# Hybrid encoder trunk on one core: split weight tiles kept in DRAM, sample attention in a pipelined order, another order at the start and at the end

## The chip, the cores and the metric

The kernel runs on one NeuronCore of one Trainium2 chip. The metric is device time in microseconds for one execution; the time before is 3031.82 us, the median of three runs (3031.12 to 3034.32). Matmuls run on TensorE (PE; its weight loads are shown as PEld), elementwise work on VectorE (DVE), ScalarE (ACT) and GpSimd (POOL). All DMAs are issued by SyncE (SP), from one queue that is worked off in order, and run on 16 DMA engines.

## The reference

One layer is computed for two groups of requests that share the weights: a prompt of 2048 tokens and a sample of 8 x 16 tokens, each of the latter with 1024 cached keys and values. All of it is in 32-bit floats.

```
h = rms_norm(x, norm_g)                                  # (tokens, 1024)
(a_x, a_b, a_c, a_z, g_q, g_f, g_i, g_z,
 s_q, s_k, s_v, s_z, m_a, m_b, m_c) = split_cols(h @ w_in)   # 12 x 512 + 3 x 1024 columns
o_a = a_b * conv3(a_c * a_x) * silu(a_z)                 # branch A: short causal convolution
o_b = rms_norm(hgrn_scan(g_q, f(g_f), k(g_f), g_i)) * silu(g_z)   # branch B: gated linear recurrence
q, k = rms_norm(s_q, q_norm_g), rms_norm(s_k, k_norm_g)  # per head, 8 heads of 64
z = q @ k.T / 8                                          # branch C: stick-breaking attention, strictly causal
A = sigmoid(z) * (product over later keys of sigmoid(-z))
o_c = (A @ v) * silu(s_z)
m = sigmoid(m_a) * (o_a @ wb_a) + sigmoid(m_b) * (o_b @ wb_b) + sigmoid(m_c) * (o_c @ wb_c)
y = x + m @ w_out
```

Outputs are y, the last convolution rows, the recurrent states, and the keys and values of both request groups.

## The kernel before

Tokens are cut into 17 tiles of 128: tile 0 is the sample, tiles 1 to 16 the prompt. The input projection goes over three token groups of 5, 6 and 6 tiles (`GROUPS`, L39), each in two chunks of at most 384 tokens. `run_jobs` (L1118) runs the same 64 jobs for each group. A job is one block of columns of w_in: a channel job (`chan_job`, L1000) has 128 columns, one weight part, and computes them channel by token (`proj_chan`, L581: 8 blocks of k, 3 matmuls each); a token job (`tok_job`, L993) has 256 columns in two parts (k blocks 0 to 3 and 4 to 7) and computes them token by channel (`proj_tok`, L593). Jobs of the first stretch alternate: one channel job, one token job of k, v or q.

**Three matmuls for a product.** Every operand is split (`split`, L174): ScalarE casts it to float32r (hi), VectorE subtracts that from the source (lo), and `PASS3` (L579) multiplies hi by hi, hi by lo and lo by hi. `wload` (L179) does this for weights: one DMA of 512 KB into a staging tile wst (2 buffers), then hi into whi and lo into wlo (3 buffers each). It is called one job ahead (L1132, L1133; L1269 to L1271 in the merge), and again for each token group, so the same 72 parts of w_in are loaded and split three times, and the 20 parts of w_branch and w_out four times.

**Start.** `Prepare` loads x, squares and sums a tile on ScalarE (`square`, L501), takes the inverse root on POOL (`rstd_of`, L192: a multiply-add and a pow), scales by it and by the gain g_bc on VectorE (`scale`, L508), transposes on TensorE and splits the result into hh and hl (`turn`, L512). For group 0 this is `first_steps` (L544). The DMA of g_bc (512 KB, broadcast to all partitions) is the first in the queue (L172). The lower bound of the forget gate (L641 to L655), seven level masks (L659 to L671) and two selectors (L808 to L815) are built at the start on POOL and VectorE.

**Keys and queries.** `post_qk` (L679) normalizes them, transposes into one PSUM bank (ps_hg, L148) and copies that on ScalarE to kt (one buffer, L701), which goes to DRAM.

**Background work.** Generators are stepped between the pieces of a job, by a budget of their yielded costs (`Background`, L58; rates at L45 to L48): the recurrence, the sample attention in group 1, the prompt attention in group 2 and the merge. The framework that turns this program into queues may also move an instruction ahead on its engine where its buffers are free.

**Sample attention** (`sample_attention`, L344): for each of 8 requests, three segments of keys, the last keys first. A segment loads 2 or 3 blocks of keys, transposes them (L405), forms z (L412), two sigmoids, the running product (scan, L424) and its product with sigmoid(z) (L426), transposes that (L429) and multiplies by the values (L447). All this stands in one row, segment after segment.

**Merge.** Four groups of tiles (`PGROUPS`, L41). For each, 12 branch jobs (`bjob`, L1200: branch x of 3, 256 output columns dp of 4) multiply by w_branch; the product is gated on VectorE (L1231, L1233), added on POOL (L1234) and, for x = 2, split into mh and ml. Four output jobs (`ojob`, L1239), each with two weight parts, multiply by w_out, add x and store y (L1253, L1254). The output jobs of a group alternate with the first four branch jobs of the next; those of the last group come alone at the end. Before the last branch, what is left of that group's attention is run out (L1207).

Of the kernel before, what the change touches and what calls it, by code (L numbers as in the profile page):

```python
# [11 lines left out]
I32 = mybir.dt.int32  # L12
# [86 lines left out]
def trunk(ctx: ExitStack, tc: tile.TileContext, x_prompt, x_sample, cache_conv, state_hgrn, cache_k, cache_v,  # L99
# [72 lines left out]
    nc.sync.dma_start(g_bc, norm_g[0].partition_broadcast(P))  # L172

    def split(hi, lo, src, eng=None):  # L174

        nc.scalar.copy(hi, src)  # L176
        (eng or nc.vector).tensor_tensor(lo, src, hi.bitcast(F32), ALU.subtract)  # L177

    def wload(pieces):  # L179

        out = []
        for v in pieces:
            a, b = v.shape[1], v.shape[2]
            st = wp.tile([P, a, b], F32, tag="wst", name="wst", bufs=2)
            nc.sync.dma_start(st, v)
            hi = wp.tile([P, a, b], F32R, tag="whi", name="whi")
            lo = wp.tile([P, a, b], F32R, tag="wlo", name="wlo")
            split(hi, lo, st)
            out.append((hi, lo))
        return out  # L190

    def rstd_of(ssq, n, count):  # L192

        v = small.tile([P, n], F32, tag=f"rv{n}", name="rv")
        nc.gpsimd.tensor_scalar(v, ssq, 1.0 / count, EPS, ALU.mult, ALU.add)
        r = small.tile([P, n], F32, tag=f"rr{n}", name="rr")
        nc.gpsimd.tensor_tensor(r, v, mhalf.broadcast_to([P, n]), ALU.pow)
        return r
# [58 lines left out]
    def attn_pair(m0, m1):  # L257
# [15 lines left out]
        for m in range(m0, m1):  # L273
# [8 lines left out]
            for i in range(nq):  # L282
# [61 lines left out]
    def sample_attention():  # L344
# [45 lines left out]
        for b in range(NB):  # L390
            pv = ps_pv()
            carry = one
            vnew = sa.tile([TS, 8, 64], F32, tag="vnew", name="vnew", bufs=1)
            nc.sync.dma_start(vnew, VV[b * TS:(b + 1) * TS])
            for sg in (2, 1, 0):
                nblk = 2 if sg == 2 else 3
                w = nblk * P + (TS if sg == 2 else 0)
                kt = sa.tile([P, 4, 384], F32, tag="kt", name="kt", bufs=2)
                for bi in range(nblk):
                    blk = 3 * sg + bi  # L400
                    kc = sa.tile([P, 512], F32, tag="cst", name="kc", bufs=3)
                    nc.sync.dma_start(kc, cache_k[0, b, blk * P:(blk + 1) * P].rearrange("t h d -> t (h d)"))
                    tp = ps_tp()
                    for h in range(4):
                        nc.tensor.transpose(tp[:, h * P:(h + 1) * P], kc[:, h * P:(h + 1) * P], idf)  # L405
                    nc.scalar.copy(kt[:, :, bi * P:(bi + 1) * P], tp.rearrange("p (h t) -> p h t", h=4))
                    yield 1.3
                z = ps_z()
                if sg == 2:
                    nc.tensor.matmul(z[:, 256:256 + TS], idb, nmask, start=True, stop=False, skip_group_check=True)  # L410
                for h in range(4):
                    nc.tensor.matmul(z[32 * h:32 * h + 32, :nblk * P], qz[:, h, b], kt[:, h, :nblk * P],  # L412
                                     start=sg != 2, stop=True, skip_group_check=True)
                if sg == 2:
                    for h in range(4):
                        nc.tensor.matmul(z[32 * h:32 * h + 32, 256:256 + TS], qz[:, h, b],
                                         knew[:, h, b * TS:(b + 1) * TS], start=False, stop=True,
                                         skip_group_check=True)
                nc.scalar.activation(sn[:, 384 - w:384], z[:, :w], AF.Sigmoid, scale=-0.125)
                sp = sa.tile([P, 384], F32, tag="sp", name="sp")  # L420
                nc.scalar.activation(sp[:, :w], z[:, :w], AF.Sigmoid, scale=0.125)
                pr = sa.tile([P, 385], F32, tag="pr", name="pr")
                s_in = sn[:, 384 - w:385][:, ::-1]
                nc.vector.tensor_tensor_scan(pr[:, 384 - w:385][:, ::-1], s_in, s_in, carry, ALU.mult, ALU.bypass)  # L424
                carry = pr[:, 384 - w:385 - w]
                nc.vector.tensor_tensor(sp[:, :w], sp[:, :w], pr[:, 385 - w:385], ALU.mult)  # L426
                tp = ps_tp()
                for bi in range(nblk):
                    nc.tensor.transpose(tp[:, bi * P:(bi + 1) * P], sp[:, bi * P:(bi + 1) * P], idf)  # L429
                at_ = sa.tile([P, 384], F32, tag="at", name="at_")  # L430
                if sg == 2:
                    nc.tensor.transpose(tp[0:TS, 256:384], sp[:, 256:256 + TS], idf)
                    nc.scalar.copy(at_[:, 0:256], tp[:, 0:256])
                    nc.scalar.copy(at_[0:TS, 256:384], tp[0:TS, 256:384])
                else:
                    nc.scalar.copy(at_, tp[:, :384])
                yield 2.0
                for bi in range(3):
                    blk = 3 * sg + bi
                    if blk == 8:  # L440
                        vc, n = vnew, TS
                    else:
                        vc, n = sa.tile([P, 8, 64], F32, tag="vst", name="vc", bufs=3), P
                        nc.sync.dma_start(vc, cache_v[0, b, blk * P:(blk + 1) * P])
                    for h in range(4):
                        c = bi * P + 32 * h
                        nc.tensor.matmul(pv[32 * h:32 * h + 32, 0:P].rearrange("p (e d) -> p e d", e=2),  # L447
                                         at_[0:n, c:c + 32], vc[0:n, 2 * h:2 * h + 2],
                                         start=sg == 2 and bi == 0, stop=sg == 0 and bi == 2, skip_group_check=True)
                    yield 0.6  # L450
            od = sa.tile([P, P], F32, tag="od", name="od", bufs=1)
            nc.scalar.copy(od, pv[:, 0:P])
            for h in range(8):
                nc.sync.dma_start(OCS[b * TS:(b + 1) * TS, h * 64:(h + 1) * 64],
                                  od[h * TS:(h + 1) * TS, 64 * (h % 2):64 * (h % 2) + 64])
            yield 1.0
# [24 lines left out]
    class Prepare:  # L481
# [30 lines left out]
        def turn(self, i, kk):  # L512
# [10 lines left out]
            split(hh[sl], hl[sl], tp.rearrange("p (k t) -> p k t", k=4))  # L523
# [20 lines left out]
        def first_steps(self):  # L544

            n = len(self.tiles)
            for i in range(n):
                self.fetch(i, xp.tile([P, D], F32, tag="xt", name="xt") if i < 2 else
                           g0p.tile([P, D], F32, tag="xt0", name="xt0", bufs=3))
            for f in (self.square, self.scale):  # L550
                for i in range(2):
                    f(i)
            self.scaled = True
            for i in range(n):
                if i > 2:
                    self.square(i)
# [747 lines left out]
```

## Time and profile before

| What | Value |
|---|---|
| time, median of 3 runs | 3031.82 us (3031.12 to 3034.32) |
| the profiled execution's own time | 3036.76 us |
| its span, first to last instruction | 3035.1 us |
| TensorE clock granted, mean | 0.991 |
| DMA traffic | 394.40 MB, mean 130 GB/s |
| HBM read, written | 303.67 MB, 87.33 MB |

How to read it: the page gives for each engine the time in which it was busy and its share of the span. A group row names a line, engine and operation, the tiles written and read, the count, the total busy time, the mean of one, and how long the engine stood idle ahead of it and what ended that. In a row of waits stand the waiting engine and line, what it waited for, the total, the number of waits and the longest. Rows of a timeline begin with the start and the duration in us; the square bracket gives the idle time before and its releaser. The granted clock is a share of TensorE's full clock. SPq is the queue of DMA issues; the time there is that of the issue, and "to landing" is the time from issue until the data is there. Matmul records overlap, as matmuls are pipelined, so the pace is read from their starts. The durations are those of one profiled execution.

### The profile page before, as it was taken

The numbers are of one execution on the slowest core, as the hardware profiler recorded it, in microseconds if no ns is written. First come the engines' busy times: TensorE is split into PE (matmuls) and PEld (weight loads), VectorE is DVE, ScalarE is ACT, GpSimd is POOL, SyncE is SP. The second block draws the span as 40 slices with busy tenths as digits, with TensorE's granted clock in tenths as the row PEclk, the third lists the DMA queues.
The fourth block names the chain that finished last, engine by engine and source line by source line (L and its number), as shares of the span: only waits on it lengthen the run. The fifth ranks groups of instructions, "written<-read, shape, count | busy, mean of one in ns | idle before, by whom it ended". The sixth has DMA issues, their size and how long they took to land. (4 is left out here: it accounts for less than half of the span.)

```text
span 3035.1 us, 51813 instructions
## 1 busy us (share of the span) xinstructions
PE 2934.7 (97%) x19609; PEld 2688.3 (89%) x19609; DVE 1759.2 (58%) x3412; ACT 1230.2 (41%) x2571; POOL 454.7 (15%) x861
## 2 busy tenths in 40 slices
PE   7999999999999999999999999999999899899998
PEld 7999999988988888999899998998998788687887
DVE  5345535652434352636635757567577877978753
ACT  4332232243333333224434444444445555555531
POOL 3110000110100000001322111111012412313211
PEclk9999999999999999999999999999999999999999
DMA  5433323455444444323444232323226455555553
GB/s 178 139 109 112 99 90 105 120 161 166 130 126 138 130 131 121 115 78 114 150 152 127 81 122 81 119 66 100 89 87 216 149 164 171 157 184 170 171 160 121
DMA packets 448842, 394.40 MB, mean 130 GB/s; under 512 B 24809, under 2 KB 388674, under 8 KB 448594
## 3 DMA queue, kind: packets, MB, share of 16 engines
q1 hardware_dynamic: 448594, 391.09, 42.3%
q8 instruction: 155, 2.54, 0.4%
q14 instruction: 93, 0.76, 0.1%
HBM read 303.67 MB, written 87.33 MB: 129 GB/s over the span
## 5 line engine op out<-in xcount | busy, mean ns | idle before, releaser
L587 PE MATMUL acc<-hh,whi 128*128 128x384 f32 (+1 forms) x2688 | 937.8, 349 | 0.5 <-ACT hh L176 0.3
L587 PE MATMUL acc<-hl,whi 128*128 128x384 f32 (+1 forms) x2688 | 887.6, 330 | 0.0
L587 PE MATMUL acc<-hh,wlo 128*128 128x384 f32 (+1 forms) x2688 | 887.5, 330 | 0.0
L177 DVE TENSOR_TENSOR wlo<-wst,whi 128x1024 fp32r<-128x1024 f32 x296 | 372.1, 1260 | 435.0 <-ACT whi L176 420.7
L587 PEld LDWEIGHTS acc<-hh,whi 128*128 128x128 f32 x2688 | 508.1, 189 | 37.3 <-issue 31.1
L587 PEld LDWEIGHTS acc<-hl,whi 128*128 128x128 f32 x2688 | 509.2, 189 | 4.9 <-issue 1.0
L587 PEld LDWEIGHTS acc<-hh,wlo 128*128 128x128 f32 x2688 | 507.3, 189 | 0.0
L176 ACT CAST whi<-wst 128x1024 fp32r<-128x1024 f32 x296 | 311.0, 1051 | 364.1 <-PE acc L587 272.4
L598 PE MATMUL acc<-whi,hh 128*128 128x256 f32 x1088 | 317.2, 292 | 7.2 <-DVE gm L986 5.0
L598 PE MATMUL acc<-wlo,hh 128*128 128x256 f32 x1088 | 308.6, 284 | 0.5 <-DVE wlo L177 0.5
L598 PE MATMUL acc<-whi,hl 128*128 128x256 f32 x1088 | 308.6, 284 | 0.0
L298 DVE TENSOR_TENSOR_SCAN pr<-snb,carry 128x513 f32<-128x513 f32 x192 | 259.4, 1352 | 74.3 <-ACT snb L289 73.2
L271 ACT COPY aT<-tp 128x512 f32<-128x512 f32 (+2 forms) x320 | 167.8, 525 | 236.3 <-PE tp L270 233.6
L303 DVE TENSOR_TENSOR sp<-sp,pr 128x512 f32<-128x512 f32 (+2 forms) x320 | 202.0, 631 | 35.1 <-POOL sp L294 13.2
L598 PEld LDWEIGHTS acc<-whi,hh 128*128 128x128 f32 x1088 | 207.2, 190 | 11.7 <-DVE gm L986 5.7
L289 ACT ACTIVATE snb<-z 128x512 f32<-128x512 f32 (+2 forms) x320 | 172.3, 539 | 90.2 <-PE z L286 85.5
L598 PEld LDWEIGHTS acc<-wlo,hh 128*128 128x128 f32 x1088 | 207.4, 191 | 0.7 <-DVE wlo L177 0.7
L598 PEld LDWEIGHTS acc<-whi,hl 128*128 128x128 f32 x1088 | 207.4, 191 | 0.4
L270 PE MATMUL tp<-idf,sp 128*128 128x128 f32 x1088 | 173.1, 275 | 15.8 <-ACT aT L271 15.1
L1225 PE MATMUL acc<-oh,whi 128*128 128x512 f32 (+2 forms) x480 | 179.8, 376 | 8.6 <-DVE gate L1233 7.1
L298 DVE TENSOR_TENSOR_SCAN pr<-snb,one 128x129 f32<-128x129 f32 (+3 forms) x128 | 114.5, 894 | 112.1 <-POOL snb L294 112.0
L291 ACT ACTIVATE sp<-z 128x512 f32<-128x512 f32 (+2 forms) x320 | 171.7, 537 | 16.9 <-DMA OX<-ot 13.0
(301 smaller groups left out, 4773.4 us busy)
## 6 DMA issues: line engine op xcount, KB each, us to landing
wst<-in_w_in_dram SPq DMA_DIRECT2D x216, 512.0 KB, 3.9
wst<-in_w_branch_dram SPq DMA_DIRECT2D x48, 512.0 KB, 4.0
GM<-gm SPq DMA_DIRECT2D x120, 192.0 KB, 2.0
Kt<-KT SPq DMA_DIRECT2D x80, 256.0 KB, 3.1
gate<-GM SPq DMA_DIRECT2D x72, 256.0 KB, 2.7
kc<-in_cache_k_dram SPq DMA_DIRECT2D x64, 256.0 KB, 2.9
vc<-in_cache_v_dram SPq DMA_DIRECT2D x64, 256.0 KB, 2.8
wst<-in_w_out_dram SPq DMA_DIRECT2D x32, 512.0 KB, 4.5
```

Source lines behind the costliest of these rows:

```text
L176: nc.scalar.copy(hi, src)
L177: (eng or nc.vector).tensor_tensor(lo, src, hi.bitcast(F32), ALU.subtract)
L270: nc.tensor.transpose(tp[:, j * P:(j + 1) * P], sp[:, j * P:(j + 1) * P], idf)
L271: nc.scalar.copy(aT[:, e, 0:nb, i * P:(i + 1) * P], tp[:, :w].rearrange("p (b q) -> p b q", q=P))
L289: nc.scalar.activation(sn[:, 512 - w:512], z[:, :w], AF.Sigmoid, scale=-0.125)
L291: nc.scalar.activation(sp[:, :w], z[:, :w], AF.Sigmoid, scale=0.125)
L298: nc.vector.tensor_tensor_scan(pr[:, 512 - w:513][:, ::-1], s_in, s_in, one if diag else carry[e][i], ALU.mult, ALU.bypass)
L303: nc.vector.tensor_tensor(sp[:, :w], sp[:, :w], pr[:, 513 - w:513], ALU.mult)
L587: nc.tensor.matmul(acc[:, :n], w[0][a][:, k], hT[b][:, k, :n], start=k == 0 and i == 0, stop=k == KB - 1 and i == 2)
L598: nc.tensor.matmul(acc[:, :256], hT[b][:, k, ti * P:(ti + 1) * P], w[k // 4][a][:, k % 4], start=k == 0 and i == 0, stop=k == KB - 1 and i ...
L1225: nc.tensor.matmul(acc[:, :n], w[0][a][:, k, dd * P:(dd + 1) * P], box[x][b][:, k, sl], start=k == 0 and i == 0, stop=k == 3 and i == 2)
```

## The change

Five things change.

1. **Weights.** hi and lo of a part lie in one tile w (1 MB, 3 buffers, as much room as whi and wlo had). After the first chunk of a job of token groups 0 and 1, and ahead of a job in the merge, `wkeep` stores each part that isn't kept yet in a DRAM tile of its own. Where a part is kept, `wload` loads hi and lo by one DMA from there, without staging and split.
2. **Sample attention.** Keys, scores, transposes and values are functions of their own, and the scores of segment m + 1 go out between the transposes and the values of segment m. The sp tiles are two fixed ones, and the new values lie in a zeroed tile of 128 rows, so that every segment turns three blocks and multiplies full blocks.
3. **Start.** g_bc is loaded after the first tile of x. The scale of the third tile comes after both splits of the first tile. The squares and scales of tiles 3 and 4 are queued behind the first weight split, and bound, masks and selectors behind that split and the last pow then issued. (`tc.issue_after(i)` queues what is traced in the block behind i, on i's engine.)
4. **End.** In the last merge group the additions of branch 2 are on VectorE, and the first output job does k blocks 0 to 5 of three tiles, then blocks 6 and 7 of them, then the fourth tile.
5. **Buffers.** kt of `post_qk` has 2 instead of 1, xr 3 instead of 2, yt 2 instead of 1, carry 9 instead of 16.

```diff
     def split(hi, lo, src, eng=None):
-        nc.scalar.copy(hi, src)
-        (eng or nc.vector).tensor_tensor(lo, src, hi.bitcast(F32), ALU.subtract)
+        first = nc.scalar.copy(hi, src)
+        return first, (eng or nc.vector).tensor_tensor(lo, src, hi.bitcast(F32), ALU.subtract)
...
+    kept = {}
+    def wload(pieces, key):
         out = []
-        for v in pieces:
+        for n, v in enumerate(pieces):
             a, b = v.shape[1], v.shape[2]
-            st = wp.tile([P, a, b], F32, tag="wst", name="wst", bufs=2)
-            nc.sync.dma_start(st, v)
-            hi = wp.tile([P, a, b], F32R, tag="whi", name="whi")
-            lo = wp.tile([P, a, b], F32R, tag="wlo", name="wlo")
-            split(hi, lo, st)
-            out.append((hi, lo))
+            w = wp.tile([P, 2, 1024], F32R, tag="w", name="w")
+            hi, lo = (w[:, i].rearrange("p (a b) -> p a b", a=a) for i in range(2))
+            if (key, n) in kept:
+                nc.sync.dma_start(w.bitcast(F32), kept[key, n].bitcast(F32))
+            else:
+                st = wp.tile([P, a, b], F32, tag="wst", name="wst", bufs=2)
+                nc.sync.dma_start(st, v)
+                pair = split(hi, lo, st)
+                if not first_split:
+                    first_split.extend(pair)
+            out.append((hi, lo, w))
         return out
+    def wkeep(out, key):
+        for n, (_, _, w) in enumerate(out):
+            if (key, n) not in kept:
+                kept[key, n] = dram.tile([P, 2, 1024], F32R, name=f"W{len(kept)}")
+                nc.sync.dma_start(kept[key, n].bitcast(F32), w.bitcast(F32))
...
-                    carry[e][i] = at.tile([P, 1], F32, tag="carry", name="carry", bufs=16)
+                    carry[e][i] = at.tile([P, 1], F32, tag="carry", name="carry", bufs=9)
...
+        def turned(m):
+            b, sg = order[m]
+            sp = held[m][0]
+            tp = ps_tp()
+            for bi in range(3):
+                nc.tensor.transpose(tp[:, bi * P:(bi + 1) * P], sp[:, bi * P:(bi + 1) * P], idf)
+            at_ = sa.tile([P, 384], F32, tag="at", name="at_")
+            nc.scalar.copy(at_, tp[:, :384])
...
+        yield from keys(0)
+        scores(0, masked(0))
+        yield 0.7
+        for m in range(last + 1):
+            if m < last:
+                yield from keys(m + 1)
+            turned(m)
+            yield 2.0
+            z = masked(m + 1) if m < last else None
+            values(m)
+            if z is not None:
+                scores(m + 1, z)
+            yield 2.2
...
+                if i == 0:
+                    nc.sync.dma_start(g_bc, norm_g[0].partition_broadcast(P))
...
                 if i > 2:
-                    self.square(i)
-                    yield
-                    self.scale(i)
-                    yield
+                    with tc.issue_after(first_split[0].ins), tc.issue_after(first_split[1].ins):
+                        self.square(i)
+                        yield
+                        self.scale(i)
+                        yield
                 for kk in range(0, KB, 4):
                     self.turn(i, kk)
                     yield
-                    if i == 0:
-                        (self.scale if kk else self.square)(2)
+                    if i == 0 and not kk:
+                        self.square(2)
+                if i == 0:
+                    with tc.issue_after(self.last[1].ins):
+                        self.scale(2)
                 self.ready = i
+                yield
...
-        kt = qk.tile([P, 4, P], F32R, tag="kt", name="kt", bufs=1)
+        kt = qk.tile([P, 4, P], F32R, tag="kt", name="kt", bufs=2)
...
+            if not g and at_ == 1:
+                with tc.issue_after(rstd_at[0].ins), tc.issue_after(first_split[1].ins):
+                    build_bound()
+                    build_masks()
+                    build_selectors()
...
+            if ci == 0 and g < len(GROUPS) - 1:
+                wkeep(ws[i], jobs[i][0][1])
...
-                            nc.gpsimd.tensor_tensor(m, m, gate[:, sl], ALU.add)
+                            (nc.vector if final and x == 2 else nc.gpsimd).tensor_tensor(
+                                m, m, gate[:, sl], ALU.add)
...
         def ojob(s):
+            cuts = [KB - 2, KB] if final and s == 0 else [KB]
             def compute(w):
...
+                for t0 in range(0, len(tiles), 3 if len(cuts) > 1 else 1):
+                    some = range(t0, min(len(tiles), t0 + (3 if len(cuts) > 1 else 1)))
+                    xrs, accs = {}, {}
+                    for c, end in enumerate(cuts):
+                        for ti in some:
+                            if not c:
+                                xrs[ti] = p3.tile([P, 256], F32, tag="xr", name="xr", bufs=3)
...
+                            for k in range(cuts[c - 1] if c else 0, end):
...
+                            yt = p3.tile([P, 256], F32, tag="yt", name="yt", bufs=2)
...
         if i + 1 < len(alljobs):
-            ws[i + 1] = wload(alljobs[i + 1][0])
+            ws[i + 1] = wload(*alljobs[i + 1][0])
+        wkeep(ws[i], alljobs[i][0][1])
```

`build_bound`, `build_masks` and `build_selectors` hold what stood at L641 to L655, L660 to L671 and L809 to L815. `keys`, `masked`, `scores` and `values` hold what stood at L398 to L407, L408 to L410, L411 to L426 and L438 to L455.

More of the change, by code (lines that the diff above doesn't have):

```diff
@@ L196, in rstd_of @@
         r = small.tile([P, n], F32, tag=f"rr{n}", name="rr")
-        nc.gpsimd.tensor_tensor(r, v, mhalf.broadcast_to([P, n]), ALU.pow)
+        rstd_at[0] = nc.gpsimd.tensor_tensor(r, v, mhalf.broadcast_to([P, n]), ALU.pow)
         return r
@@ L389, in sample_attention @@
         yield 1.0
[L390 to L410, printed above, removed]
-                for h in range(4):
[L412 to L456, printed above, removed]
@@ new lines, in sample_attention, with blocks, keys @@
+        order = [(b, sg) for b in range(NB) for sg in (2, 1, 0)]
+        held = {}
+        pvs = {}
+        sps = [single([P, 384], F32, f"sps{i}") for i in range(2)]
+        for x in sps:
+            nc.gpsimd.memset(x, 0.0)
+        vnew = single([P, 8, 64], F32, "vnew")
+        nc.gpsimd.memset(vnew, 0.0)
+        def blocks(m):
+            return 2 if order[m][1] == 2 else 3
+        def keys(m):
+            b, sg = order[m]
+            kt = sa.tile([P, 4, 384], F32, tag="kt", name="kt", bufs=2)
+            for bi in range(blocks(m)):
+                blk = 3 * sg + bi
+                kc = sa.tile([P, 512], F32, tag="cst", name="kc", bufs=3)
+                nc.sync.dma_start(kc, cache_k[0, b, blk * P:(blk + 1) * P].rearrange("t h d -> t (h d)"))
+                tp = ps_tp()
+                for h in range(4):
+                    nc.tensor.transpose(tp[:, h * P:(h + 1) * P], kc[:, h * P:(h + 1) * P], idf)
+                nc.scalar.copy(kt[:, :, bi * P:(bi + 1) * P], tp.rearrange("p (h t) -> p h t", h=4))
+                yield 1.3
+            held[m] = [kt]
@@ new lines, in turned @@
+        def turned(m):
+            b, sg = order[m]
+            sp = held[m][0]
+            tp = ps_tp()
+            for bi in range(3):
+                nc.tensor.transpose(tp[:, bi * P:(bi + 1) * P], sp[:, bi * P:(bi + 1) * P], idf)
+            at_ = sa.tile([P, 384], F32, tag="at", name="at_")
+            nc.scalar.copy(at_, tp[:, :384])
+            vs = []
+            for bi in range(blocks(m)):
+                blk = 3 * sg + bi
+                vc = sa.tile([P, 8, 64], F32, tag="vst", name="vc", bufs=3)
+                nc.sync.dma_start(vc, cache_v[0, b, blk * P:(blk + 1) * P])
+                vs.append(vc)
+            if sg == 2:
+                nc.sync.dma_start(vnew[0:TS], VV[b * TS:(b + 1) * TS])
+                vs.append(vnew)
+            held[m] += [at_, vs]
@@ new lines, in values @@
+        def values(m):
+            b, sg = order[m]
+            at_, vs = held[m][2:4]
+            if sg == 2:
+                pvs[b] = ps_pv()
+            pv = pvs[b]
+            for bi, vc in enumerate(vs):
+                for h in range(4):
+                    c = bi * P + 32 * h
+                    nc.tensor.matmul(pv[32 * h:32 * h + 32, 0:P].rearrange("p (e d) -> p e d", e=2),
+                                     at_[:, c:c + 32], vc[:, 2 * h:2 * h + 2],
+                                     start=sg == 2 and bi == 0, stop=sg == 0 and bi == 2, skip_group_check=True)
+            if sg == 0:
+                od = sa.tile([P, P], F32, tag="od", name="od", bufs=1)
+                nc.scalar.copy(od, pv[:, 0:P])
+                for h in range(8):
+                    nc.sync.dma_start(OCS[b * TS:(b + 1) * TS, h * 64:(h + 1) * 64],
+                                      od[h * TS:(h + 1) * TS, 64 * (h % 2):64 * (h % 2) + 64])
@@ L457, in sample_attention @@
+        last = len(order) - 1
+        yield from keys(0)
[11 more added lines that the diff above has]
+            yield 2.2
         oc = sa.tile([P, 512], F32, tag="cst", name="oc", bufs=3)
@@ L1125, in weights @@
             if i < n and i not in ws:
[L1126 removed]
+                ws[i] = wload(*jobs[i][0])
         order = [(i, ci) for i in range(2, n - 2) for ci in range(2)]
```

138 lines of the change are left out of this document (84 added, 54 removed).

## The prediction

> **What bounds the kernel now.** I read the page's busy shares first, then the busy time by stage, then what TensorE waited for, then the granted clock around its longest waits.
>
> ```profile
> span 3035.1 us, 51813 instructions
> ...
> PE 2934.7 (97%) x19609; PEld 2688.3 (89%) x19609; DVE 1759.2 (58%) x3412; ACT 1230.2 (41%) x2571; POOL 454.7 (15%) x861
> ```
>
> TensorE is the bound: 100.4 us of the span are not covered by a matmul, and no other engine is near. What the change takes off VectorE and ScalarE counts only where one of them made TensorE wait. By stage (the columns are the stretch, its length, busy time of PE, PEld, DVE, ACT and POOL with the number of instructions, clock, DMA share, GB/s):
>
> ```profile
> 20.00:610.00 590.00, 581.24 (x4163) 572.33 (x4162) 289.67 (x766) 181.69 (x396) 52.27 (x112) 0.99 0.38 113
> 610.00:1400.00 790.00, 772.11 (x5517) 712.99 (x5516) 344.09 (x833) 263.82 (x579) 47.92 (x95) 0.99 0.43 128
> 1400.00:2290.00 890.00, 873.85 (x5620) 811.49 (x5618) 562.84 (x1111) 417.22 (x935) 151.98 (x350) 0.99 0.36 110
> 2290.00:3036.00 746.00, 703.24 (x4298) 588.04 (x4298) 554.62 (x687) 358.85 (x649) 190.25 (x272) 0.98 0.53 165
> ```
>
> Group 0 loses 8.8 us, group 1 (with the sample attention) 17.9, group 2 16.2, the merge 42.8. The rest, some 15 us, is the start. What ended TensorE's waits (total, times, longest), and one wait of ScalarE:
>
> ```profile
> PE tp L521 <- DVE xt L510: 12.5, 3, 10.9
> PE tp L429 <- DVE sp L426: 11.0, 21, 2.3
> PE tp L521 <- DVE hl L177: 7.6, 5, 3.1
> PE hg L700 <- ACT kt L702: 7.4, 6, 2.3
> ...
> PE acc L1247 <- ACT mh L176: 5.7, 3, 2.7
> ```
>
> ```profile
> ACT kt L702 <- DMA KT<-kt: 54.3, 23, 4.5
> ```
>
> A wait costs more than its length, as the clock shows in six stretches right behind such waits (three in the sample attention, two behind L700, one at the end):
>
> ```profile
> 670.00:673.40 3.40, 3.40 (x15) 3.16 (x13) 1.09 (x3) 1.56 (x3) 0.00 (x0) 0.50 0.53 174
> ...
> 707.60:711.00 3.40, 2.68 (x9) 2.17 (x7) 0.43 (x2) 0.78 (x2) 0.00 (x0) 0.50 0.54 182
> ...
> 810.00:813.40 3.40, 3.40 (x18) 3.40 (x18) 0.42 (x1) 1.10 (x3) 0.19 (x1) 0.50 0.79 230
> ...
> 1509.70:1513.10 3.40, 3.22 (x14) 3.22 (x15) 1.24 (x4) 0.82 (x5) 0.54 (x2) 0.50 0.93 280
> ...
> 1639.40:1642.80 3.40, 3.40 (x17) 3.22 (x16) 0.24 (x1) 1.68 (x5) 0.54 (x2) 0.50 0.35 114
> 2978.00:2980.80 2.80, 0.55 (x3) 0.30 (x2) 0.94 (x2) 0.42 (x1) 1.26 (x1) 1.00 0.84 276
> 2980.80:2991.00 10.20, 7.10 (x29) 6.50 (x30) 3.54 (x5) 1.76 (x3) 2.11 (x1) 0.50 0.27 79
> ```
>
> At clock 0.50 the stretch of 3.4 us costs about 1.7 us more, and the 10.2 us at the end about 5.1. The Trainium skill, "TensorE: Matmul & The Clock Gate", Part 1, says the clock falls to half after at least one idle window of about 3.4 us. By that rule no wait of at most 2.3 us costs clock, and the 8.5 us that I count as clock for L429 and L700 below would not come back. The trace disagrees: the waits before the first five stretches are no longer than 2.3 us, and each is followed by 0.50. I go by the trace.
>
> **The change, part by part.** *Start.*
>
> ```profile
> 6.42 1.06 ACT L505 ACTIVATE junk<-xt 128x1024 bf16<-128x1024 f32 x1 [4.36 <-DMA xt<-in_x_sample_dram]
> ...
> 7.90 1.06 POOL L809 MEMSET qblk<- 128x1152 f32 x1
> ...
> 8.93 0.57 POOL L197 TENSOR_TENSOR rr<-rv,mhalf 128x1 f32<-128x1 f32 x1
> ...
> 9.53 1.28 DVE L510 SCALAR_TENSOR_TENSOR xt<-xt,rr,g_bc 128x1024 f32<-128x1024 f32 x1 [7.59 <-POOL rr L197]
> ...
> 22.56 0.67 PE L587 MATMUL acc<-hh,whi 128*128 128x384 f32 x1
> ```
>
> The first tile of x is queued on SP behind the 512 KB of g_bc. At the rate of the DMA rows below (138 GB/s at a share of 0.44, so 313 GB/s at full share) those take 1.7 us, which x now gains. The memset of qblk, which stands ahead of the pow, leaves (1.06 us). One scale of 1.28 us leaves VectorE's queue ahead of the first two hl. Sum 4.0 us on the path to the first product; about another 1 us from the squares of tiles 3 and 4 that leave ScalarE's queue ahead of the first product (at 22.56 now). I take -5. g_bc lands later, but behind one tile only. The moved builds of masks, bound and selectors run on POOL and VectorE beside projections (POOL is busy 52 of 590 us in group 0); if they delay a pow of rstd_of, the k post-processing behind it waits and then TensorE for an accumulator. Bounds -8 and +2.
>
> *Stores of the parts in group 0.*
>
> ```profile
> wst<-in_w_in_dram SPq DMA_DIRECT2D x216, 512.0 KB, 3.9
> wst<-in_w_branch_dram SPq DMA_DIRECT2D x48, 512.0 KB, 4.0
> ...
> wst<-in_w_out_dram SPq DMA_DIRECT2D x32, 512.0 KB, 4.5
> ```
>
> ```profile
> 76.00:152.00 76.00, 74.91 (x599) 74.69 (x599) 25.38 (x47) 24.44 (x49) 8.75 (x15) 1.00 0.44 138
> ```
>
> 216 loads over three groups are 72 parts a group; 72 stores of 1 MB in 590 us add 128 GB/s, a share of 0.41 to the 0.38. It fits, beside TensorE's work, as an average. A slot of w is now also held until its store has read it, and ScalarE's next cast waits for that, with evacuations queued behind it. I take +2; bounds 0 (hidden) and +12.
>
> *Sample attention.* The scores of a segment go out one segment ahead, so the transposes of sp no longer stand right behind scan and product. That removes L429's 11.0 us and three half-clock stretches, 5.1: 16.1. VectorE's chain now lies beside the next segment's key transposes and the projections in between; were that cover gone, the wait would come back whole. The matmuls are the same in number (rows of zeros fill the short block). I leave 2 us for new waits: -14; bounds -16 and -5.
>
> *kt with two buffers.* ScalarE's copy waited for the store of the copy before (54.3 us), and TensorE for the one bank that this copy frees: 7.4 us and two half-clock stretches, 3.4. Sum 10.8; I take -9, as the bank stays single; bounds -11 and -3.
>
> *Groups 1 and 2 load finished parts.* A load was 0.5 MB and is 1 MB, and it waits on SP for a slot that TensorE frees, where a staging buffer freed earlier had served.
>
> ```profile
> SPq L185 <- DVE wlo L177: 333.1, 148, 17.2
> ```
>
> SP already stands up to 17.2 us in front of a weight load, with attention loads and gate stores queued behind, so this wait changes its releaser more than its length. A 1 MB load is in no row: 3.9 us plus 0.5 MB at 313 GB/s, 1.7, gives an estimate of 5.6 us; the bounds are 4.5 (the w_out row, were rows of 8 KB free) and 7.3 (a full 1 MB at that rate, 3.4, on top of 3.9). A job of channels in these groups runs 48 matmuls of 384 columns; 24 of 256 take 2.85 us:
>
> ```profile
> 2660.85 2.85 PE acc L1247 x24
> ```
>
> so by columns 8.5 us, and the fetch hides under one job. 144 splits leave VectorE and ScalarE there, worth little, as few of TensorE's waits in these groups are theirs. I take +1; bounds -6 and +14.
>
> *Merge, groups 1 to 3.* Here VectorE does matter, in two stretches where x = 2 begins:
>
> ```profile
> 2590.00:2660.00 70.00, 61.16 (x310) 45.37 (x310) 62.02 (x68) 36.12 (x66) 22.82 (x22) 0.98 0.53 167
> ...
> 2780.00:2830.00 50.00, 42.09 (x188) 32.19 (x187) 40.91 (x49) 23.77 (x51) 24.12 (x35) 0.90 0.49 155
> ```
>
> ```profile
> 2607.05 2.30 DVE L177 TENSOR_TENSOR wlo<-wst,whi 128x1024 fp32r<-128x1024 f32 x1
> ```
>
> TensorE loses 8.8 + 7.9 = 16.7 us idle and 1.4 + 5 = 6.4 of clock, while VectorE is 89% and 82% busy. Each stretch holds four to six subtractions like the one shown, about 10 us of VectorE that go. What is late next is the POOL addition and the attention's own scan, so I take half: -12; bounds -20 and 0. Merge group 0 still splits, and stores 12 MB in some 150 us, +84 GB/s (48 branch loads over four groups are 12 parts each): +3; bounds 0 and +8. The smaller buffer counts cost nothing: at most eight carries are live and a ninth is written, the scan that read the slot's last one having ended before. The third xr and the second yt only free SP and VectorE of waits at the end.
>
> *End.*
>
> ```profile
> 2978.25 0.68 DVE L1233 TENSOR_TENSOR gate<-acc,gate 128x512 f32<-128x512 f32 x1
> ```
>
> ```profile
> 2982.46 2.11 POOL L1234 TENSOR_TENSOR mp<-mp,gate 128x512 f32<-128x512 f32 x1 [2.12 <-DVE gate L1233]
> ```
>
> The last additions move to VectorE (about 0.7 us, like the product over 512 columns, for 2.11), and the first output job does blocks 0 to 5 of three tiles first: 54 matmuls, 6.4 us, that need nothing of the last two blocks. That covers L1247's 5.7 us and the 5.1 of clock: -11; bounds -12 and -8. But the last three output jobs follow one another, two parts each on three slots: the second part of the next one goes into the slot of k blocks 0 to 3, which is read until half a tile (1.4 us) before the job's end, and it is needed 1.4 us into the next. 5.6 - 2.8 leaves 2.8 us three times, 8.4, and one half-clock stretch: +10; bounds +4 and +16. The Trainium skill, "DMA: Bandwidth & Descriptors", Bandwidth, gives 6.15 us for a load of 1 MB. By it the three stalls make 10 us and the sum is 1.6 us higher; no run shows such a load yet.
>
> Sum: -5 + 2 - 14 - 9 + 1 - 12 + 3 - 11 + 10 = -35. The profiled execution took 3036.76 us (the span and 1.7 around it), which gives 3002; the median of the runs is 4.9 us below it, so 2997.
>
> **Rivals.** *Weights arrive late.* From group 1 on, 204 parts (144, and in the merge three times 12 and 8, as 48 and 32 loads are over four groups) come as 1 MB into slots that TensorE frees, on one in-order queue. For it: the queue stands on L185 for 333.1 us already, and behind the w load wait the loads of attention. Against it: 8.5 us of cover for 5.6. It decides once the queue holds some 3 us (0.9 MB) ahead of the load; 0.4 us a part is then +82, against -35: 3079; at 0.2 us, 3038. *The waits move.* The sample attention, the k path and the merge stretches give half (17 of 35 us lost again): 3014. *More is given.* The output jobs at the end find their weights in time (-10) and the VectorE-bound stretches heal (-8): 2979. *The storing brings nothing by itself:* parts that take as long to fetch as to split would leave the merge terms at 0 and the rest as it is: 3009, within the second rival's reach.
>
> **How the numbers follow.** The sum as worked out (2985 to 3010) 0.58; more is given 0.14; the waits move, or the storing brings nothing (3010 to 3030) 0.17; weights late 0.11, of which 0.02 ends about where it began. Within 0.2%, 6 us, is about what a measurement of this kernel cannot tell from no change. Faster is 0.58 + 0.14 + 0.13 = 0.85, same 0.04 + 0.02 = 0.06, slower 0.09. The range leaves out the slow case and the far end of the good one: 2970 to 3028.
>
> **What would show it.** First product before 19 us (22.6 now). No L429-like wait over 1 us and no half clock between 640 and 900. L700's wait below 2 us. PE idle in group 0 not above 11 us. In the merge, less than 10 us idle where x = 2 begins. At the end, three gaps of 2 to 3 us, released by a DMA into w, where the L1247 waits stood. The forecast is wrong if matmuls of groups 1 and 2 wait for DMA into w by more than 10 us in all, or if DMA shares in group 0 pass 0.9.

## The result and the profile after

| What | Before | After |
|---|---|---|
| time, median | 3031.47 us (3030.66 to 3034.32, 4 runs) | 2947.77 us (2944.85 to 2957.94, 4 runs) |
| ratio, 95% interval | | 0.9728 (0.9703 to 0.9753) |
| the profiled execution | 3036.76 us | 2945.98 us |
| DMA traffic | 394.40 MB | 597.81 MB |

The change made the kernel 84 us faster. The forecast was 2997, with a range that ended at 2970: right in sign, and less than half of the size.

The page of the changed kernel begins like this:

```profile
span 2944.3 us, 51331 instructions
...
PE 2885.2 (98%) x19609; PEld 2675.8 (91%) x19609; DVE 1538.6 (52%) x3216; ACT 1038.9 (35%) x2359; POOL 426.1 (14%) x856
```

TensorE executes the same 19609 matmuls, but its busy time fell by 49.5 us, from 2934.7. A forecast that looks for gains in TensorE's idle time alone cannot find these. To see where they lie, here are the stages of both kernels at their true borders (start, group 0, 1, 2, merge, and the end behind the last branch product); the columns are those of the windows in the prediction. Before:

```profile
0.00:22.60 22.60, 5.86 (x25) 4.66 (x25) 10.62 (x21) 10.94 (x18) 13.97 (x39) 1.00 0.82 260
22.60:611.00 588.40, 580.64 (x4165) 572.14 (x4163) 287.65 (x763) 179.72 (x394) 50.97 (x106) 0.99 0.38 114
611.00:1413.70 802.70, 784.80 (x5598) 725.21 (x5597) 349.82 (x843) 271.09 (x597) 49.16 (x98) 0.99 0.43 127
1413.70:2281.00 867.30, 852.89 (x5493) 793.89 (x5492) 547.80 (x1092) 401.94 (x904) 147.90 (x343) 0.99 0.36 108
2281.00:2974.40 693.40, 660.25 (x3952) 543.57 (x3951) 544.96 (x668) 358.43 (x655) 187.20 (x272) 0.99 0.55 171
2974.40:3035.10 60.70, 50.24 (x384) 48.86 (x384) 18.39 (x29) 8.05 (x9) 5.50 (x3) 0.92 0.36 115
```

After:

```profile
0.00:18.10 18.10, 6.20 (x26) 4.76 (x26) 8.35 (x17) 9.04 (x15) 4.20 (x15) 1.00 0.82 276
18.10:601.10 583.00, 576.60 (x4168) 569.01 (x4169) 289.68 (x766) 180.51 (x396) 56.19 (x133) 1.00 0.76 249
601.10:1354.30 753.20, 751.01 (x5593) 727.01 (x5592) 268.53 (x770) 200.52 (x515) 47.57 (x98) 1.00 0.56 185
1354.30:2205.20 850.90, 844.99 (x5493) 789.80 (x5492) 470.05 (x1022) 339.90 (x833) 146.50 (x343) 1.00 0.47 155
2205.20:2891.90 686.70, 659.84 (x3954) 539.65 (x3954) 491.18 (x623) 307.69 (x602) 171.65 (x267) 1.00 0.72 241
2891.90:2944.30 52.40, 46.57 (x384) 45.57 (x383) 10.84 (x23) 1.24 (x2) 0.00 (x0) 0.99 0.59 205
```

Between the two profiled executions, which are 90.8 us apart in span, the start gives 4.5 us, group 0 5.4, group 1 49.5, group 2 16.4, the merge 6.7, the end 8.3. More than half comes from group 1, the stage with the sample attention. There TensorE's idle time went from 17.9 to 2.2 us, and the half clock, worth 5.1 us, is gone. But its busy time fell by 33.8 us (784.80 to 751.01) with the same matmuls; even if all 5.1 of the clock lay in it, 28.7 us vanished from time that the profile calls busy.

What TensorE still waits for, and the two new DMAs (KB each, us to landing):

```profile
PE tp L287 <- ACT aT L288: 8.5, 5, 2.6
PE acc L1315 <- DVE gate L1323: 4.1, 7, 1.1
PE acc L1347 <- DMA w<-W: 3.6, 6, 1.0
...
PE acc L671 <- DMA w<-W: 1.0, 2, 0.7
```

```profile
w<-W SPq DMA_DIRECT2D x204, 1024.0 KB, 5.3
W<-w SPq DMA_DIRECT2D x92, 1024.0 KB, 5.4
```

The waits at L429 and L700, 18.4 us before, have no successor (their lines are now L473 and L778). The stored weights are hardly ever late: 1.0 us in groups 0 to 2. The load of 1 MB lands after 5.3 us, close to the estimate of 5.6.

### The profile page after: what moved, and what is told of

Same layout as the page of the kernel before. It is cut to its first block, busy times and chain, and to the rows that moved or that the text cites. A ratio compares the mean times of both kernels' runs of the same rounds, so it can differ in the third digit from the quotient of the medians.

```text
span 2944.3 us, 51331 instructions
## 1 busy us (share of the span) xinstructions
PE 2885.2 (98%) x19609; PEld 2675.8 (91%) x19609; DVE 1538.6 (52%) x3216; ACT 1038.9 (35%) x2359; POOL 426.1 (14%) x856
## 2 busy tenths in 40 slices
DMA packets 326407, 597.81 MB, mean 203 GB/s; under 512 B 26281, under 2 KB 228354, under 8 KB 288274
## 5 line engine op out<-in xcount | busy, mean ns | idle before, releaser
L660 PE MATMUL acc<-hh,w 128*128 128x384 f32 (+1 forms) x5376 | 1465.7, 338 | 1.4 <-ACT w L175 0.8
L660 PEld LDWEIGHTS acc<-hh,w 128*128 128x128 f32 x5376 | 966.1, 188 | 25.9 <-issue 17.9
L660 PE MATMUL acc<-hl,w 128*128 128x384 f32 (+1 forms) x2688 | 885.4, 329 | 0.0
L660 PEld LDWEIGHTS acc<-hl,w 128*128 128x128 f32 x2688 | 507.9, 189 | 4.9 <-issue 1.0
L671 PE MATMUL acc<-w,hh 128*128 128x256 f32 x2176 | 412.4, 285 | 4.1 <-DVE gm L1066 2.3
L671 PEld LDWEIGHTS acc<-w,hh 128*128 128x128 f32 x2176 | 341.6, 188 | 6.3 <-DVE gm L1066 2.4
L671 PE MATMUL acc<-w,hl 128*128 128x256 f32 x1088 | 306.5, 282 | 0.0
L1315 PE MATMUL acc<-oh,w 128*128 128x512 f32 (+1 forms) x960 | 294.1, 367 | 5.6 <-DVE gate L1323 4.1
L1347 PE MATMUL acc<-w,mh 128*128 128x256 f32 x1088 | 212.3, 285 | 4.8 <-DMA w<-W 3.6
L671 PEld LDWEIGHTS acc<-w,hl 128*128 128x128 f32 x1088 | 205.1, 189 | 0.4
L308 ACT ACTIVATE sp<-z 128x512 f32<-128x512 f32 (+2 forms) x320 | 171.9, 537 | 13.9 <-DMA OX<-ot 7.9
```

The lines of the kernel that those rows point to most:

```text
L660: nc.tensor.matmul(acc[:, :n], w[0][a][:, k], hT[b][:, k, :n], start=k == 0 and i == 0, stop=k == KB - 1 and i == 2)
L671: nc.tensor.matmul(acc[:, :256], hT[b][:, k, ti * P:(ti + 1) * P], w[k // 4][a][:, k % 4], start=k == 0 and i == 0, stop=k == KB - 1 and i ...
L1315: nc.tensor.matmul(acc[:, :n], w[0][a][:, k, dd * P:(dd + 1) * P], box[x][b][:, k, sl], start=k == 0 and i == 0, stop=k == 3 and i == 2)
L1347: nc.tensor.matmul(acc[:, :256], box["l" if b else "h"][:, k, ti * P:(ti + 1) * P], w[k // 4][a][:, k % 4], start=k == 0 and i == 0, stop= ...
```

## Experiments

**What makes busy time vanish.** The timeline of TensorE before, where the values of a segment (L447) come between two products (start, duration, then the group):

```profile
860.46 0.34 PE L587 MATMUL acc<-hl,whi 128*128 128x384 f32 x1
860.63 0.34 PE L587 MATMUL acc<-hh,wlo 128*128 128x384 f32 x1
860.90 0.42 PE L447 MATMUL pv<-vc,at__9592 128*32 128x128 f32 x8
861.26 0.44 PE L587 MATMUL acc<-hh,whi 128*128 128x384 f32 x1
```

The starts count, since records overlap. One product follows another after 0.17 us (860.46, 860.63); the first matmul of the values comes 0.27 after the last product, and the next product 0.36 after it, though eight of these small matmuls take only 0.21 when they stand in a long row (26 ns apart on average). Their tile has 32 columns of weights (128\*32), that of the products 128. After the change, a segment's values and the next segment's scores stand in one row:

```profile
740.72 0.34 PE L660 MATMUL acc<-hh,w 128*128 128x384 f32 x1
740.99 0.64 PE L496 MATMUL pv<-vc,at__8496 128*32 128x128 f32 x16
741.45 0.40 PE L496 MATMUL pv<-vnew,at__8496 128*32 128x128 f32 x8
741.66 0.83 PE L450 MATMUL z<-kt,qz 128*32 128x384 f32 x8
```

Counted over the whole trace, 32-column matmuls come in 97 runs before (scores and three blocks of values for each of 24 segments, and one for the queue's own order) and in 25 after. The old code yields to the projection behind each block of values; the new code does not. **Theory 1:** each run costs some 0.3 us at its two ends, hidden in the busy time; 72 runs fewer are 20 to 25 us. **Theory 2:** the matmuls of group 1 go faster because the splits of 72 weight parts have left VectorE and ScalarE.

*The new sample attention alone*, in the kernel before (the function is exchanged, nothing else):

```diff
-        for b in range(NB):
-            pv = ps_pv()
-            carry = one
...
+        order = [(b, sg) for b in range(NB) for sg in (2, 1, 0)]
+        held = {}
+        pvs = {}
...
```

> The kernel before with nothing changed but the sample attention, which is the new one. Theory 1 (the 0.3 us that TensorE loses each time it goes into and out of a run of 32-column matmuls, hidden in its busy time): group 1 goes from 802.7 to about 757 us, from idle time and clock by about 18 us and from about 72 fewer runs by 23; the whole by 40 to 48 us. Theory 2 (the matmuls of group 1 go faster because 72 splits of weights are gone from VectorE and ScalarE, the 16 of idle time and clock apart): 12 to 20 us in all, and the intervals between products in group 1 stay as before. Group 2, the merge and the end stay within 4 us of before by both.

Measured: 0.9888 of before (0.9873 to 0.9903), 34 us less. Group 1:

```profile
607.40:1374.70 767.30, 754.75 (x5599) 729.26 (x5598) 349.01 (x843) 267.92 (x589) 48.82 (x98) 1.00 0.43 133
```

VectorE is as busy as before (349 us, all splits are there), yet TensorE's busy time is 30 us lower. Theory 2 falls. The whole is 34 and not 40 to 48, in part because waits for the bank of `post_qk` grew (7.4 to 11.2 us), of which more below.

*Three runs in place of one*, in the kernel after:

```diff
+                if bi < 2:
+                    yield 0.75
...
-            values(m)
+            yield from values(m)
...
-            yield 2.2
+            yield 0.7
```

> The kernel after, with the matmuls of the values in three runs for each segment in place of one: a yield of 0.75 behind each of the first two blocks, and 0.7 in place of 2.2 at the end. Same matmuls, same data, 48 more runs. Theory 1: 48 times 0.3 us, 14 us more (10 to 18), all of it in group 1 and with no more idle time on TensorE than now. Theory 2: within 3 us of after.

Measured: 2962.25 us, 0.9779 (0.9765 to 0.9794) against 0.9728, 15 us more. Group 1, with 75 runs in the whole trace:

```profile
600.20:1371.40 771.20, 767.96 (x5592) 723.95 (x5592) 268.85 (x770) 200.06 (x514) 47.55 (x98) 1.00 0.55 181
```

17.0 us more of busy time for 50 runs more, 0.34 us a run, and only 1 us of idle time.

*One run in the kernel before:*

```diff
-                    yield 0.6
+                yield 1.8
```

> The kernel before, with the values of a segment in one run: its three yields of 0.6 become one of 1.8 behind the three blocks. Theory 1: 14 us less than before (10 to 18), in group 1, while the waits for the product ahead of the transposes (11.0 us) and their half clock stay. Theory 2: within 3 us of before.

Measured: 0.9966 (0.9954 to 0.9977), 10 us less. Group 1:

```profile
611.40:1401.90 790.50, 769.22 (x5598) 726.86 (x5597) 349.11 (x843) 270.71 (x597) 49.17 (x98) 1.00 0.42 129
```

The busy time falls by 15.6 us (13.9 without the clock's part) for 48 runs, 0.29 a run; the waits at L429 are still 11.0 us. A single moved `yield` gives a third of a per cent.

The first experiment has 25 runs to these 49, and 12.8 us less busy time, again without the clock's part. At 0.3 a run, 24 runs are 7 of these. Of the other 6, some 3.5 are part of the waits at L429 that the profile counts as busy. The step from the start of a product to the transposes of sp, idle time not counted, is 338 ns in 21 places here and 173 in 20 there: the record of the product ahead lasts 0.34 us, where the next matmul could start after 0.17. The last 2 us or so stay open.

*Full shape*, with three runs: is it the shape, or any interruption?

```diff
-                    nc.tensor.matmul(pv[32 * h:32 * h + 32, 0:P].rearrange("p (e d) -> p e d", e=2),
-                                     at_[:, c:c + 32], vc[:, 2 * h:2 * h + 2],
+                    nc.tensor.matmul(pv[:, h * P:(h + 1) * P].rearrange("p (e d) -> p e d", e=2),
+                                     at_[:, bi * P:(bi + 1) * P], vc[:, 2 * h:2 * h + 2],
```

> The kernel of the three runs with the matmuls of the values in full shape: 128 columns of weights in place of 32, each into a stretch of 128 columns of the bank of its own, of which the rows that are wanted are copied at the end (four copies in place of one for each request). Same values, 288 matmuls at about 110 ns apart in place of 26: 24 us more in group 1 by the rows alone. Theory 1 in its narrow form (the 0.3 us is for the change between full and 32-column shapes): no cost for the three runs any more, group 1 at about 777 us, the whole 24 us above after. Rival (any run of float32 matmuls put between float32r products costs it, whatever its shape): 14 us more on top, group 1 at 791, the whole 38 above after.

Measured: 2994.57 us, 47 above after, which neither theory said. My count was wrong: each of these 288 float32 products stands as two matmuls in the trace, 576, and 576 times 84 to 87 ns is 48 to 50 us. Group 1:

```profile
599.90:1402.20 802.30, 800.24 (x5592) 777.50 (x5592) 268.76 (x770) 206.63 (x538) 47.66 (x98) 1.00 0.53 174
```

With the right count the narrow form gives 799 to 801 of busy time, the rival 14 more; it is 800.24. The timeline says it directly:

```profile
745.53 0.34 PE L662 MATMUL acc<-hh,w 128*128 128x384 f32 x1
745.70 1.05 PE L495 MATMUL pv<-vc,at__8499 128*128 128x128 f32 x8
746.51 0.42 PE L662 MATMUL acc<-hh,w 128*128 128x384 f32 x1
```

The way into a run now takes 0.17 us, as between two products, and the last small matmul is left after 31 ns (median of 49). It is the change between the tile shapes that costs.

**Storing.** *No stores*, so every part is loaded and split each time (`wkeep` keeps nothing):

```diff
-            if (key, n) not in kept:
+            if False:
```

> The kernel after without the stores: no part is kept, so every part is loaded and split for each token group, as before the change. Theory 1: group 1 stays within 4 us of after (753.2 us); the merge groups 1 to 3 lose about the 10 us they had gained, merge group 0 and group 0 get 3 to 5 back; in all 3 to 12 us more than after. Theory 2: group 1 becomes about 25 us longer, and the whole 30 to 40.

Measured: 2957.14 us, 0.9768 (0.9752 to 0.9784): storing gives 12 us by the ratios, and 9.4 by the spans of the two profiled executions. Groups 0, 1, 2, merge and end:

```profile
18.10:596.00 577.90, 575.41 (x4162) 567.91 (x4163) 290.06 (x767) 181.30 (x396) 58.09 (x133) 1.00 0.39 117
596.00:1353.40 757.40, 753.25 (x5599) 729.36 (x5598) 351.40 (x843) 268.48 (x587) 49.32 (x98) 1.00 0.44 135
1353.40:2209.80 856.40, 846.33 (x5493) 789.66 (x5492) 548.49 (x1092) 403.14 (x904) 147.41 (x343) 1.00 0.36 110
2209.80:2903.40 693.60, 661.97 (x3954) 544.70 (x3954) 551.56 (x676) 358.21 (x656) 176.72 (x267) 0.99 0.54 171
2903.40:2953.70 50.30, 45.90 (x385) 45.48 (x383) 18.15 (x29) 7.97 (x9) 0.00 (x0) 1.00 0.42 134
```

Against after, the stores cost group 0 5.1 us and the end 2.1; they give 4.2 in group 1, 5.5 in group 2 and 6.9 in the merge. Group 1 has its low busy time here too, with all splits: theory 2 falls a second time.

*Only w_branch and w_out stored*, and *only w_in stored*:

```diff
-            if ci == 0 and g < len(GROUPS) - 1:
+            if False:
                 wkeep(ws[i], jobs[i][0][1])
```

> The kernel after that stores only the parts of w_branch and w_out; those of w_in are loaded and split for each token group. By the stages of the run without any store: group 0 about 5 us shorter than after, group 1 about 4 and group 2 about 5 longer, the merge as after: 2 to 7 us more in all. Rival (the stores of w_in pay for nothing, the gain of storing is all in the merge): within 2 us of after or below it.

```diff
-        wkeep(ws[i], alljobs[i][0][1])
```

> The kernel after that stores only the parts of w_in; the merge loads and splits its parts four times. Merge group 0 about 1 us shorter than after, groups 1 to 3 about 8 longer, the end about 2 shorter: 3 to 8 us more than after, and groups 0 to 2 as after. Rival (the merge term was all a gain of other parts): within 2 us of after.

Measured: 0.9748 (0.9734 to 0.9762) and 0.9745 (0.9731 to 0.9759), 6 and 5 us above after by the ratios. Their intervals overlap that of after, so that it is the stages that speak. Without the stores of w_in, group 0 took 579.6 us, 3.4 less than after, and groups 1 and 2 took 756.5 and 857.5, 9.9 more. Without those of the merge, the merge took 694.2 us, 7.5 more, and the end 50.9, 1.5 less. So each half brings some 6 us, as both forecasts said and their rivals did not.

**The other parts, undone one by one in the kernel after.** *kt with one buffer:*

```diff
-        kt = qk.tile([P, 4, P], F32R, tag="kt", name="kt", bufs=2)
+        kt = qk.tile([P, 4, P], F32R, tag="kt", name="kt", bufs=1)
```

> The kernel after with one buffer for the kt of post_qk again. If the term of -9 us in the prediction holds, 9 us more than after (3 to 11), by waits of TensorE for the bank behind ScalarE's copy of 7 us in all and half clock behind some of them. Rival: in the changed kernel this wait is covered, and it is within 2 us.

Measured: 2968.97 us, 0.9797 (0.9770 to 0.9824), 21 us more, where 3 to 11 were expected. Groups 0, 1 and 2 are longer by 4.4, 12.8 and 6.5 us:

```profile
18.00:605.40 587.40, 579.01 (x4168) 570.63 (x4169) 289.91 (x766) 180.45 (x396) 56.62 (x133) 1.00 0.74 246
605.40:1371.40 766.00, 755.57 (x5592) 730.55 (x5592) 268.77 (x770) 199.56 (x514) 48.03 (x98) 0.99 0.55 183
1371.40:2228.80 857.40, 846.38 (x5494) 789.64 (x5492) 469.98 (x1022) 339.18 (x833) 148.11 (x343) 1.00 0.47 154
```

TensorE waits 12.6 us at this bank, 7.4 in the kernel before, and its longest wait there is 4.0 us, 2.3 before. The row of ScalarE just ahead of that longest wait, TensorE's own, and 4.7 us behind it:

```profile
797.67 0.59 ACT L780 CAST kt<-hg 128x512 fp32r<-128x512 f32 x1 [5.88 <-DMA QT<-kt]
```

```profile
798.31 0.75 PE L778 MATMUL hg<-idr,st 128*128 128x128 f32 x4 [4.04 <-ACT kt L780]
```

```profile
798.30:803.00 4.70, 4.69 (x24) 4.69 (x25) 1.99 (x5) 1.68 (x4) 1.20 (x2) 0.50 0.53 160
```

ScalarE stands 5.9 us for the store of the last copy, with everything it would do for TensorE queued behind; the 4.0 us of idle time come with 6.8 us at half clock. With one buffer the change would have given 63 us, not 84.

*The old end* (additions on POOL, the first output job tile by tile, two xr, one yt):

```diff
-            cuts = [KB - 2, KB] if final and s == 0 else [KB]
+            cuts = [KB]
...
-                            (nc.vector if final and x == 2 else nc.gpsimd).tensor_tensor(
+                            nc.gpsimd.tensor_tensor(
```

> The kernel after with the end of before: the additions of branch 2 on POOL, the first output job one tile after another, two xr and one yt; the stored weights stay. If the term of -11 us holds: 8 to 12 us more than after, all of it in the last stretch, with two or three waits of about 2 us for POOL's additions and a half clock behind them. Rival: the late weights hide it, and it is 2 to 5 us.

Measured: 2959.07 us, 0.9766 (0.9752 to 0.9781), 11 us more; the last stretch:

```profile
2893.40:2960.10 66.70, 52.30 (x385) 50.52 (x384) 10.38 (x22) 1.85 (x3) 3.82 (x3) 0.90 0.50 176
```

14.3 us longer than 52.40, in the longest of the four executions. Two waits for ScalarE's mh, which comes behind POOL's addition, are there as expected, but they are 2.9 us in all and not 5.7 as before. TensorE's waits for a DMA into w in this stretch rise from 2.7 to 5.4 us, 2.3 the longest, and the clock is at 0.90, which is some 7 us.

*The old start* (g_bc first, builds at once, nothing queued behind the first split):

```diff
     g_bc = const.tile([P, D], F32, name="g_bc")
+    nc.sync.dma_start(g_bc, norm_g[0].partition_broadcast(P))
...
-                with tc.issue_after(rstd_at[0].ins), tc.issue_after(first_split[1].ins):
-                    build_bound()
-                    build_masks()
-                    build_selectors()
```

> The kernel after with the start of before (g_bc loaded first; bound, masks and selectors built at the start; squares and scales of tiles 3 and 4 not queued behind the first split). The term of the start says 4.5 us more than after, all of it ahead of the first product (22.6 us in place of 18.1). Rival: the moved builds cost time later in group 0, and undoing them gives 2 to 4 us back, so that it comes within 2 us of after.

Measured: 2950.62 us, 0.9739 (0.9725 to 0.9754), 3 us more. Start and group 0:

```profile
0.00:22.70 22.70, 5.79 (x24) 4.60 (x25) 10.55 (x21) 10.88 (x18) 13.93 (x39) 1.00 0.81 259
22.70:603.80 581.10, 577.34 (x4171) 569.90 (x4170) 287.18 (x762) 178.90 (x393) 51.40 (x110) 1.00 0.75 248
```

4.6 us lost ahead of the first product, 1.9 won back in group 0: the moved builds may cost a little there, but this is no more than group 0 varies between kernels that share it (by about 3 us).

**Fewer runs still.** *Two segments in one run:* keys and transposes of two segments, then both values and the scores of the next two.

```diff
-            z = masked(m + 1) if m < last else None
-            values(m)
-            if z is not None:
-                scores(m + 1, z)
+            zs = [masked(n) for n in (m + 2, m + 3) if n <= last]
+            for n in (m, m + 1):
+                values(n)
+            for n, z in zip((m + 2, m + 3), zs):
+                scores(n, z)
```

> The kernel after with the values of two segments and the scores of the next two in one run of 32-column matmuls: 13 runs in place of 25 (value tiles six in place of three, two requests in two halves of a bank). Theory 1: 12 runs fewer at 0.27 us make group 1 about 3 us shorter, at 750 us. Against it: the second pair of sigmoids waits on ScalarE for the scan of the first (one tile sns), and copies that TensorE needs stand behind it; 1 us a pair would take it all back, 12 us.

Measured: 0.9734 (0.9719 to 0.9749), the same as after. 13 runs; group 1:

```profile
598.50:1355.60 757.10, 751.71 (x5598) 730.53 (x5598) 268.86 (x771) 200.95 (x515) 50.04 (x99) 1.00 0.55 185
```

Busy time less the clock's loss is 750.0 us, 1.0 below after, and 3.2 us more of idle time stand against it. The 3 us that were expected are not saved: between the scores of two segments the starts are 304 ns apart, nearly as much as the 416 of the way back to a product. My reading is that the last matmuls of a run, which have nothing beside them, are most of its price, and that joining two rows of scores, over 384 columns each, does not spare them. No version here beats the changed kernel.

## Why the prediction was wrong

| Part | Predicted, us | Measured, us |
|---|---|---|
| start | -5 | -3 |
| sample attention | -14 | -34, done alone |
| kt with two buffers | -9 | -21 |
| stores and loads of parts (+2, +1, -12, +3, +10) | +4 | -12 |
| order of the end | -11 | -11 |
| sum | -35 | -81; all together -84 |

The measured column is the difference of ratios times 3031; by the two intervals each is uncertain by 5 to 11 us, so that the start's alone could be nothing; its 4.6 us ahead of the first product are seen in the trace. The smaller number of carry buffers was not undone by itself.

**The step that failed first is the sample attention term:** "The matmuls are the same in number", with -16 as its bound. The 16.1 us of waits and clock did go, but the other half of the gain was never idle time. I took TensorE's busy time for work that the change leaves alone and asked only which waits end. The rows of before showed it: 0.27 us into a run and 0.36 until the next product, where eight such matmuls need 0.21. And the diff showed the cause: the three yields behind the blocks of values are gone. Two experiments, with 48 and 50 runs less and more, put a price of 0.29 to 0.34 us on a run, and a third showed that it hangs on the tile's shape.

**The kt term had the right mechanism and half the size.** I counted the waits of before at L700, with their half clock. But a wait that is removed has to be priced in the kernel that remains: undone there, the same wait is 12.6 us. The first experiment points the same way: with only the sample attention changed, these waits grew from 7.4 to 11.2 us, all of it in group 1 (1.3 to 5.8), and with the one moved `yield` they were 4.3 there. That the faster stage leaves ScalarE less time for the store is my reading, not shown; the runs show the growth. I also bounded it by TensorE's waits on that one bank, while ScalarE's stand delays its other work too: in group 0, which is 4.4 us longer, no wait of TensorE names this bank, but its waits for ScalarE's casts of w and its copies of kn and kt come to 4.3 us, 0.8 in the changed kernel.

**Storing was mis-sized by 16 us** by the ratios, by 13 by the stages. The merge (-9 by my two terms) was -6.9, and group 0 +2 was +3 to +5. Groups 1 and 2, which I put at +1, gave 9.7 us: I had written that few of TensorE's waits there are VectorE's or ScalarE's, and yet in group 2 idle time is 5.9 us with the stores and 10.1 without. The end was the largest error in this part. Three waits of 2.8 us and a clock drop, +10, were foretold; here they are:

```profile
2908.27 0.39 PE L1347 MATMUL acc<-w,mh 128*128 128x256 f32 x1 [0.97 <-DMA w<-W]
2920.70 0.39 PE L1347 MATMUL acc<-w,mh 128*128 128x256 f32 x1 [0.66 <-DMA w<-W]
2933.28 0.38 PE L1347 MATMUL acc<-w,mh 128*128 128x256 f32 x1 [0.80 <-DMA w<-W]
```

2.4 us, released as foretold, and no half clock. The three loads landed 5.9, 5.7 and 5.5 us after their issue, as assumed, but the cover was 4.7 to 5.1 us and not 2.8. In the order that the framework made, TensorE does the first half of the second tile and half of that of the third before the second half of the first. I had read the order of the work from the program's loops.

What held: the first product before 19 us (18.1), no wait behind the product of scan and sigmoid, clock 1.00 in group 1, no wait for kt, and idle time in group 0 at 6.4 us (11 foretold as the most). The DMA share in group 0 was 0.76, and 0.87 in its first 82 us. Where x = 2 begins in the merge, TensorE's idle time is 9.6 us in all, 16.7 before and 16.3 without the stores; less than 10 were foretold. Weights late, the slow rival, did not come: TensorE waited 1.0 us for them in groups 1 and 2 together and 4.2 in the merge and at the end, where the rival had 0.2 to 0.4 for each of 204 parts.

The size of the end's -11 held too, but by some luck, as its parts were others: the old end costs the changed kernel 2.9 us at mh and 2.7 more at the late weights, with some 7 us of clock where 5.1 were foretold.

The Trainium skill's rule in "TensorE: Matmul & The Clock Gate", Part 1, that the clock falls only after about 3.4 us of idle time, was set against the trace for the term of the clock. The runs side with the trace: with the waits of at most 2.3 us at L429 and L700 gone, so was the half clock in group 1, and in the run with one kt a wait of 2.3 us has 3.4 us at half clock behind it.

## What to carry to other kernels

A busy TensorE is not a working one: read the distance between starts at every change of tile shape, and keep matmuls of narrow tiles in one row, since each interruption by full ones cost 0.3 us that no list of waits shows. A wait in a queue that others stand behind should be priced by what it would be in the kernel after the other changes, not by its row in the kernel before. And where a transfer is to be covered, count the cover in the engine's own order of instructions, not in the loops of the program.

## What the runs showed of the hardware

A matmul of 32 columns behind a full one starts 93 ns later than a full one would (268 ns in place of 175 behind a product over 384 columns, 204 in place of 110 behind one over 128). On the way back, the next full product starts 203 ns behind the last small one, while matmuls of 32 columns, four column groups side by side, start every 26 ns on average, and a full matmul over 128 columns every 110. The 64-column tiles of the prompt attention (`pv`, L332) show the same: 268 in, 203 out. Full tiles of float32 between float32r products cost nothing of the kind: 0.17 us on the way in, as between two products, and 31 ns on the way back.
